# Differential attention stage: the second map is scaled on ScalarE, and its weights are split on ScalarE and VectorE instead of VectorE and GpSimd

## The chip, the core and the metric

The kernel runs on one core of one Trainium2 chip. The metric is device time in microseconds of one execution; the kernel before takes 766.11 us (median of 3 runs, 764.81 to 767.35). In the profile's names PE is TensorE's matmul stream and PEld its weight loads, DVE is VectorE, ACT is ScalarE, POOL is GpSimd and SP is the engine that issues the DMAs.

## The reference

One decoder layer on a sequence of 512 tokens, width 1024, in float32. The input is RMS-normalised and projected; two attention branches follow, latent attention with 8 heads ("MLA") and differential attention with 4 heads ("diff"). Each branch is projected to 1024 channels and multiplied by a sigmoid gate. The sum goes through an output projection and a residual; a SwiGLU feed-forward block with its own residual and a final norm end the layer. The part that the change touches is this one:

```python
o1 = causal_attention(dq[..., 0, :], dk[..., 0, :], dv)
o2 = causal_attention(dq[..., 1, :], dk[..., 1, :], dv)
lam = exp(sum(lambda_q1 * lambda_k1)) - exp(sum(lambda_q2 * lambda_k2)) + lambda_init
o_diff = rmsnorm(o1 - lam * o2, diff_subln_g) * (1.0 - lambda_init)
gates = sigmoid(gate_pre + b_gate)
merged = g_mla * (o_mla @ w_branch_mla) + g_diff * (o_diff @ w_branch_diff)
```

## The kernel before

**Numbers in two parts.** TensorE multiplies in the type float32r, which holds fewer bits than float32. Each operand is therefore kept as a rounded high part and a low part (the rest), and `mm3` (lines 298 to 302) issues three matmuls for one product: high by high (L300), high by low (L301), low by high (L302).

**Weights.** `weights` (from L270) loads a block of up to 128 x 1024 numbers by DMA into a `raw` tile (four buffers), and makes a `w` tile (three buffers) from it: `round_hi` (L261) writes the high part, `round_lo` (L267) subtracts it from the raw numbers to get the low part. A list of two names, `w_eng`, says which engine does which. In the first part of the program it is `['act', 'pool']`. From the MLA heads on it is `['dve', 'pool']`: the high part is a cast on VectorE at L265, the low part a subtraction on GpSimd at L268. In the feed-forward block it is `['act', 'dve']`: ScalarE at L263 and VectorE at L268. A block feeds 24 matmuls of 512 columns, and its buffer can be written again when the last of them is through.

**The differential heads.** `diff_head` goes over four blocks of 128 query rows; block i has (i+1) x 128 key columns. `scores` (from L623) makes both maps of a block on TensorE (L632) into two PSUM buffers (`ps_sc`, just two). VectorE adds the mask and takes the row maximum (L636), which writes the map to a `P` tile in SBUF and frees the PSUM buffer; ScalarE takes the exponential and its row sum (L155); VectorE takes the reciprocal of the sum (L639). Then the second map is multiplied by its reciprocal and by minus lambda (L684, VectorE), and the first map, multiplied by its own reciprocal, is added to it (L685, VectorE). TensorE transposes the result (L658), and the values are multiplied in `values` (L669). `diff_norm` (from L699) normalises a head; its sums over partitions run on TensorE (L703).

**What else runs there.** While the heads run, `fill` puts projections between their matmuls: those of the later diff heads (`diff_qk`, whose rotary part uses L563 and L564 on VectorE and L565 and L566 on GpSimd) and of the gates (`gate`, emptied from PSUM at L487). When all heads are through, `sigmoids` runs 16 sigmoids on ScalarE (L494), with a load of the function table ahead of them and one behind. Then come the branch projections: `branch(0, m)` and `branch(1, m)` for m = 0, 2, 4, 6, each from one block of weights; L797 multiplies a result with its gate.

**What sets the order.** Each engine works through its own list in order. The lists are written by a scheduler ahead of the run, by its own estimates of the durations and with priorities (`urgent` puts a head's work first); waits between the engines are semaphores. So another duration or another engine for one instruction can change the lists of all engines.

Of the kernel before, what the change touches and what calls it, by code (L numbers as in the profile page):

```python
# [16 lines left out]
AF = mybir.ActivationFunctionType  # L17
ALU = mybir.AluOpType
# [28 lines left out]
P_POOL = (0, 1)  # L47
W_ENG0 = ['act', 'pool']
W_ENG = ['dve', 'pool']
FILL = [[("gate", 0, 0)], [], [("pe", 0), ("mr", 0), ("gate", 0, 1), ("mv", 0)]]  # L50
FILL_MLA = [[("mqk", 1), ("mr", 1), ("v", 0), ("pe", 1)],
            [("mqk", 2), ("mr", 2), ("v", 1), ("mv", 1)],
# [40 lines left out]
def build(ctx, nc, tc, a, out):  # L93
# [9 lines left out]
    def T(tag, shape, dtype):  # L103
        return sb.tile(shape, dtype, name=nm(tag), tag=tag, bufs=BUFS[tag])
# [4 lines left out]
    def L_():  # L109
        return T("L", [P, 2, S], F32R)  # L110
# [4 lines left out]
    def tmp():  # L115
        return T("t", [P, S], F32)
# [4 lines left out]
    def r32(ap):  # L121
        return ap.bitcast(F32)
# [136 lines left out]
    w_eng = list(W_ENG0)  # L259
# [130 lines left out]
    neg_lam = sb.tile([P, 1], F32, name="neg_lam")  # L390
# [32 lines left out]
    for src in (turn_c, turn):  # L423
        tg = tmp()
        nc.gpsimd.memset(tg, 0.0)
        for q in range(4):
            with tc.issue_after(last_sin.ins):
                last_sin = nc.scalar.activation(out=tg[32 * q:32 * q + 32, q * P:(q + 1) * P],
                                                in_=src[32 * q:32 * q + 32, :], func=AF.Sin, scale=TWO_PI)
# [22 lines left out]
    def latent_norm(b):  # L452
        c0, ncol = ((0, QR), (QR, KVR))[b]
        nc.vector.tensor_mul(out=lat_ss[b], in0=lat_ss[b], in1=x_ms)
        rs = rsqrt(lat_ss[b], ncol, NB)
        nc.vector.tensor_mul(out=rs, in0=rs, in1=x_rs)
        for t in range(NB):
            l = latn[t][:, c0:c0 + ncol]
            nc.vector.tensor_scalar(out=l, in0=l, scalar1=rs[:, t:t + 1], scalar2=None, op0=ALU.mult)
            if b == 1:  # L460
                l = latn[t][:, c0 + ncol:c0 + ncol + RD]
                nc.vector.tensor_scalar(out=l, in0=l, scalar1=x_rs[:, t:t + 1], scalar2=None, op0=ALU.mult)
# [4 lines left out]
    def latents(n):  # L467
        for b in range(len(lat), n):
            pt = PS("tr")
            for t in range(NB):  # L470
                nc.tensor.transpose(out=pt[:, t * P:(t + 1) * P], in_=latn[t][:, b * P:(b + 1) * P], identity=ident)
            l = L_()
            split(pt, l[:, 0, :], l[:, 1, :], col(R_QG + b))
            lat.append(l)
# [25 lines left out]
    def fill(work):  # L500
        for kind, *args in work:
            if kind == "gate":
                gate(*args)
            elif kind == "v":
                diff_v(*args)
            elif kind == "qk":
                qk[args[0]] = diff_qk(*args)
            elif kind == "pe":
                pe[args[0]] = mla_pe(*args)
            elif kind == "mv":  # L510
                mv[args[0]] = mla_v(*args)
            elif kind == "mqk":
                mqk[args[0]] = mla_qk(*args)
            elif kind == "mr":
                mla_rope(args[0], mqk[args[0]], pe[args[0] // 2])
# [36 lines left out]
    latent_norm(1)  # L552
    fill(FILL[0])

    latents(5)
    fill(FILL[1])

# [56 lines left out]
    def rope_key():  # L614
        pt = PS("tr")
        for t in range(NB):
            nc.tensor.transpose(out=pt[0:RD, t * P:(t + 1) * P], in_=latn[t][:, 640:672], identity=ident)
        kpe = L_()[0:RD]
        rope(pt[0:RD, :], kpe[:, 0, :], kpe[:, 1, :], cos_m, sin_m, shuf_m, 1.0, RD)
        return kpe  # L620


    def scores(maps, i):  # L623


        n = (i + 1) * P
        pss = [PS("sc") for _ in maps]
        last = len(maps[0][0]) - 1
        for j in range(last + 1):
            for ps, (products, _) in zip(pss, maps):  # L630
                q, k = products[j]
                nc.tensor.matmul(out=ps[:, :n], lhsT=q[:, i * P:n], rhs=k[:, 0:n], start=j == 0, stop=j == last)  # L632
        rs = []
        for ps, (_, m) in zip(pss, maps):
            neg_max, s, r = sm(), sm(), sm()
            nc.vector.tensor_tensor_reduce(out=m, in0=ps[:, :n], in1=mask[:, S - n:], scale=-1.0, scalar=3.4e38,  # L636
                                           op0=ALU.add, op1=ALU.min, accum_out=neg_max)
            last_exp[0] = log_exp(out=m, in_=m, func=AF.Exp, bias=neg_max, scale=-1.0, accum_out=s)
            nc.vector.reciprocal(out=r, in_=s)  # L639
            rs.append(r)  # L640
        return rs

    def prob_tiles():
        c = T("P", [P, S], F32)
        yield c[:, 0:P]
        yield c[:, P:3 * P]
        for i in (2, 3):
            yield T("P", [P, S], F32)[:, :(i + 1) * P]

    def transposed(blocks):  # L650

        pt = T("PT", [P, 2, 1280], F32R)
        for js in ((0,), (1,), (2, 3)):
            ps = PS("tr")
            c = 0
            for j in js:
                for i in range(j, NB):
                    nc.tensor.transpose(out=ps[:, c:c + P], in_=blocks[i][:, j * P:(j + 1) * P], identity=ident)  # L658
                    c += P
            o0 = OFF[js[0]]  # L660
            split(ps[:, :c], pt[:, 0, o0:o0 + c], pt[:, 1, o0:o0 + c])
        return pt

    def values(pt, v):

        ps = PS("pv")
        for n_, (vs, s) in enumerate(((0, 0), (0, 1), (1, 0))):
            for j in range(NB):
                nc.tensor.matmul(out=ps[:, j * P:S], lhsT=v(j, vs), rhs=pt[:, s, OFF[j]:OFF[j] + S - j * P],  # L669
                                 start=n_ == 0 and j == 0, stop=n_ == 2 and j == NB - 1)  # L670
        return ps
# [7 lines left out]
    def diff_head(h, products):  # L679
        blocks = []  # L680
        for i, p1 in enumerate(prob_tiles()):
            p2 = T("P", [P, S], F32)[:, :(i + 1) * P]
            r1, r2 = scores(list(zip(products, (p1, p2))), i)
            nc.vector.tensor_scalar(out=p2, in0=p2, scalar1=r2, scalar2=neg_lam, op0=ALU.mult, op1=ALU.mult)  # L684
            nc.vector.scalar_tensor_tensor(out=p1, in0=p1, scalar=r1, in1=p2, op0=ALU.mult, op1=ALU.add)  # L685
            blocks.append(p1)
        pt = transposed(blocks)
        ps = values(pt, lambda j, s: dv[(h // 2) * 2 + j // 2][:, s, (j % 2) * 256 + (h % 2) * P:
                                                              (j % 2) * 256 + (h % 2) * P + P])
        o32, sq = tmp(), tmp()  # L690
        nc.scalar.activation(out=o32, in_=ps, func=AF.Copy)
        nc.scalar.activation(out=sq, in_=ps, func=AF.Square)
        sqs = L_()
        sqs = [sqs[:, 0, :], sqs[:, 1, :]]
        nc.vector.tensor_copy(out=sqs[0], in_=sq)
        nc.gpsimd.tensor_sub(out=sqs[1], in0=sq, in1=r32(sqs[0]))
        return o32, sqs

    def diff_norm(o32, sqs):  # L699

        ps = PS("tr")
        for s in range(2):
            nc.tensor.matmul(out=ps, lhsT=ones_r, rhs=sqs[s], start=s == 0, stop=s == 1)  # L703
        y, u = tmp(), tmp()
        log_exp(out=y, in_=ps, func=AF.Ln, scale=1.0 / P, bias=eps)
        last_exp[0] = log_exp(out=y, in_=y, func=AF.Exp, scale=-0.5)
        nc.vector.scalar_tensor_tensor(out=u, in0=ps, scalar=P * EPS, in1=y, op0=ALU.add, op1=ALU.mult)
        nc.vector.scalar_tensor_tensor(out=u, in0=u, scalar=-0.5 / P, in1=y, op0=ALU.mult, op1=ALU.mult)
        nc.gpsimd.tensor_mul(out=o32, in0=o32, in1=y)
        nc.vector.scalar_tensor_tensor(out=u, in0=u, scalar=1.5, in1=o32, op0=ALU.add, op1=ALU.mult)  # L710
        o = L_()
        split(u, o[:, 0, :], o[:, 1, :], col(R_SG))
        return o
# [88 lines left out]
    kpe = rope_key()  # L802
    fill(FILL[2])
    o_mla = []
    for p in range(4):
        o = L_()
        o_mla.append(o)
        w_eng[:] = W_ENG
        fill(FILL_MLA[p])
# [3 lines left out]


    o_diff, parts = [], []
    for h in range(4):
        fill(FILL_DIFF[h])
        with urgent():
            if h > 0:
                o_diff.append(diff_norm(*parts[h - 1]))  # L820
            parts.append(diff_head(h, qk[h]))
# [176 lines left out]
```

## Time and profile before

| | us |
|---|---|
| median of 3 runs | 766.11 |
| the profiled execution's own time | 765.69 |
| its span, from the first to the last instruction | 763.9 |
| PE busy | 738.9 (97%) |
| DVE busy | 430.5 (56%) |
| ACT busy | 293.4 (38%) |
| POOL busy | 166.9 (22%) |

The 1.8 us between the execution's time and its span lie outside the instructions. A share over the whole span hides the stages: from about 420 us on, the feed-forward block keeps TensorE busy and the others half idle, while in the stretch from 150 to 290 us, where the last MLA heads and the four diff heads run, VectorE is nearly always busy. A matmul's record is longer than the distance to the next one, so that a short wait of TensorE does not show as idle time. Where a row names a releaser behind an arrow, it is the instruction that ended the wait.

### The profile page before, as it was taken

The page shows a single profiled execution, that of the slowest core. Times are in us where ns is not written, and L with a number is a line of the kernel's source. Part 1 is how long each engine was busy: PE and PEld are TensorE (multiplying, and loading weights), DVE is VectorE, ACT ScalarE, POOL GpSimd, SP SyncE. Part 2 cuts the span into 40 slices and gives each one's busy share as a digit, 9 for nine tenths or more (in the row PEclk, how much of TensorE's full clock was granted, in tenths as well). Part 3 has the DMA queues.
Part 4 walks back from the last instruction along what each step waited for, and adds up shares of the span by engine and source line. Part 5 has one row for each costly group of instructions (what it writes and reads, how often), then busy time and mean ns, then how long its engine had stood idle before and what let it go on. Part 6 is the DMA issues. An engine that isn't in the chain of part 4 may idle for free.

```text
span 763.9 us, 9613 instructions
## 1 busy us (share of the span) xinstructions
PE 738.9 (97%) x3639; PEld 620.5 (81%) x3639; DVE 430.5 (56%) x800; ACT 293.4 (38%) x567; POOL 166.9 (22%) x120
## 2 busy tenths in 40 slices
PE   7999999999898999999999999999999999999996
PEld 5888889887686788888889888888888888888885
DVE  6968698898999983578363333233323332213424
ACT  7464658554333421724243323222222223122314
POOL 3404343564664454430000000000000000000302
PEclk9999999999999999999999999999999999999999
DMA  9405343632422322327422332323232323232302
GB/s 305 113 1 133 88 122 88 151 85 58 108 70 69 84 83 82 111 87 254 102 83 73 94 110 83 110 83 111 83 110 83 111 83 110 85 108 84 111 0 110
DMA packets 99819, 76.72 MB, mean 100 GB/s; under 512 B 6303, under 2 KB 86973, under 8 KB 99773
## 3 DMA queue, kind: packets, MB, share of 16 engines
q1 hardware_dynamic: 99773, 76.12, 34.0%
q8 instruction: 28, 0.46, 0.2%
q14 instruction: 18, 0.15, 0.1%
HBM read 69.81 MB, written 2.10 MB: 94 GB/s over the span
## 4 chain that ended last, share of the span: by engine, by line
PE 80%; DVE 13%; issue 2%; ACT 1%; POOL 1%; DMA 1%; SPq 0%; DVEq 0%; POOLq 0%; ACTq 0%
PE ps_mm L301 22%; PE ps_mm L302 22%; PE ps_mm L300 22%; PE ps_sc L632 2%; DVE L L256 2%; PE ps_sc L300 1%; PE ps_sc L301 1%; PE ps_tr L301 1%; PE ps_tr L300 1%; PE ps_tr L302 1%; PE ps_sc L302 1%; DVE L L254 1%; PE ps_tr L658 1%; DVE w L265 1%; DVE P L684 1%
## 5 line engine op out<-in xcount | busy, mean ns | idle before, releaser
L302 PE MATMUL ps_mm<-X,w 128*128 128x512 f32 (+1 forms) x568 | 217.6, 383 | 0.0
L300 PE MATMUL ps_mm<-X,w 128*128 128x512 f32 (+1 forms) x568 | 217.3, 383 | 0.2 <-DVE t L564 0.2
L301 PE MATMUL ps_mm<-X,w 128*128 128x512 f32 (+1 forms) x568 | 217.3, 383 | 0.0
L268 DVE TENSOR_TENSOR w<-raw,w 128x1024 fp32r<-128x1024 f32 x66 | 82.3, 1248 | 161.1 <-ACT w L263 161.0
L263 ACT ACTIVATE w<-raw 128x1024 fp32r<-128x1024 f32 (+1 forms) x72 | 74.0, 1029 | 160.1 <-issue 78.9
L268 POOL TENSOR_TENSOR w<-raw,w 128x1024 fp32r<-128x1024 f32 (+3 forms) x48 | 102.5, 2139 | 118.3 <-DVE w L265 36.3
L300 PEld LDWEIGHTS ps_mm<-X,w 128*128 128x128 f32 x568 | 107.1, 189 | 20.3 <-DVE t L564 0.4
L301 PEld LDWEIGHTS ps_mm<-X,w 128*128 128x128 f32 x568 | 107.2, 189 | 19.9 <-DVE X L254 0.2
L302 PEld LDWEIGHTS ps_mm<-X,w 128*128 128x128 f32 x568 | 107.1, 189 | 20.0 <-POOL w L268 0.3
L933 POOL TENSOR_TENSOR L<-L,P 128x512 f32<-128x512 f32 (+1 forms) x9 | 11.5, 1297 | 410.2 <-ACT t L932 410.1
L155 ACT ACTIVATE P<-P,sm 128x128 f32<-128x128 f32 (+3 forms) x64 | 35.9, 561 | 60.1 <-DVE sm L636 59.9
L907 DVE TENSOR_TENSOR t<-t,ps_mm 128x512 f32<-128x512 f32 x22 | 15.1, 688 | 59.7 <-PE ps_mm L302 59.7
L632 PE MATMUL ps_sc<-L,L 96*128 96x128 f32 (+7 forms) x160 | 38.0, 334 | 8.7 <-DVE sm L636 8.6
L906 ACT ACTIVATE t<-ps_mm 128x512 f32<-128x512 f32 x22 | 13.2, 598 | 80.8 <-PE ps_mm L302 80.8
L632 PEld LDWEIGHTS ps_sc<-L,L 96*128 96x128 f32 (+1 forms) x160 | 26.1, 191 | 14.6 <-DVE sm L636 12.3
L301 PE MATMUL ps_mm<-w,L 128*128 128x512 f32 (+1 forms) x100 | 37.2, 372 | 0.0
L300 PE MATMUL ps_mm<-w,L 128*128 128x512 f32 (+1 forms) x100 | 37.2, 374 | 0.0
L302 PE MATMUL ps_mm<-w,L 128*128 128x512 f32 (+1 forms) x100 | 37.1, 373 | 0.0
L265 DVE CAST w<-raw 128x1024 fp32r<-128x1024 f32 (+3 forms) x42 | 35.9, 855 | 1.6 <-PE ps_mm L302 1.1
L250 ACT ACTIVATE L<-t 64x512 fp32r<-64x512 f32 (+2 forms) x47 | 29.1, 624 | 17.0 <-POOL t L566 7.4
L301 PE MATMUL ps_mm<-L,w 128*128 128x512 f32 x90 | 35.5, 394 | 0.0
L254 DVE TENSOR_TENSOR L<-t,L 128x512 fp32r<-128x512 f32 (+2 forms) x37 | 33.1, 896 | 4.0 <-ACT L L250 3.7
(264 smaller groups left out, 1269.0 us busy)
## 6 DMA issues: line engine op xcount, KB each, us to landing
raw<-w_in SPq DMA_DIRECT2D x28, 512.0 KB, 4.0
raw<-w_ffn_gate SPq DMA_DIRECT2D x22, 512.0 KB, 3.9
raw<-w_ffn_up SPq DMA_DIRECT2D x22, 512.0 KB, 3.9
raw<-w_ffn_down SPq DMA_DIRECT2D x22, 512.0 KB, 3.6
L<-L SPq DMA_DIRECT2D x32, 128.0 KB, 2.3
raw<-w_out SPq DMA_DIRECT2D x8, 512.0 KB, 3.6
L<-x SPq DMA_DIRECT2D x8, 256.0 KB, 5.1
raw<-w_branch_mla SPq DMA_DIRECT2D x4, 512.0 KB, 3.4
```

Of the source, the lines that this page charges most:

```text
L155: return nc.scalar.activation(**kw)
L250: nc.scalar.activation(out=hi, in_=src, func=AF.Copy, scale=scale)
L254: nc.vector.tensor_sub(out=lo, in0=src, in1=r32(hi))
L256: nc.vector.scalar_tensor_tensor(out=lo, in0=src, scalar=scale, in1=r32(hi), op0=ALU.mult, op1=ALU.subtract)
L263: nc.scalar.activation(out=o, in_=i, func=AF.Copy)
L265: nc.vector.tensor_copy(out=o, in_=i)
L268: (nc.vector if w_eng[1] == 'dve' else nc.gpsimd).tensor_sub(out=o, in0=i, in1=r32(hi))
L300: nc.tensor.matmul(out=o, lhsT=lh, rhs=rh, start=start, stop=False)
L301: nc.tensor.matmul(out=o, lhsT=lh, rhs=rl, start=False, stop=False)
L302: return nc.tensor.matmul(out=o, lhsT=ll, rhs=rh, start=False, stop=stop)
L632: nc.tensor.matmul(out=ps[:, :n], lhsT=q[:, i * P:n], rhs=k[:, 0:n], start=j == 0, stop=j == last)
L907: nc.vector.tensor_mul(out=g, in0=g, in1=ps)
```

## The change

The second map is scaled in two steps. VectorE multiplies the 128 reciprocals by minus lambda (one column), and ScalarE multiplies the map by that column. From the program's first diff head on, `w_eng` is `['act', 'dve']`: 26 blocks of weights (18 of the projections between the heads, 8 of the branches) get their high part on ScalarE and their low part on VectorE.

```diff
@@ -47,6 +47,7 @@
 P_POOL = (0, 1)
 W_ENG0 = ['act', 'pool']
 W_ENG = ['dve', 'pool']
+W_ENG_DIFF = ['act', 'dve']
@@ -681,7 +682,8 @@
         for i, p1 in enumerate(prob_tiles()):
             p2 = T("P", [P, S], F32)[:, :(i + 1) * P]
             r1, r2 = scores(list(zip(products, (p1, p2))), i)
-            nc.vector.tensor_scalar(out=p2, in0=p2, scalar1=r2, scalar2=neg_lam, op0=ALU.mult, op1=ALU.mult)
+            nc.vector.tensor_mul(out=r2, in0=r2, in1=neg_lam)
+            nc.scalar.activation(out=p2, in_=p2, func=AF.Copy, scale=r2)
             nc.vector.scalar_tensor_tensor(out=p1, in0=p1, scalar=r1, in1=p2, op0=ALU.mult, op1=ALU.add)
             blocks.append(p1)
@@ -813,6 +815,7 @@
     o_diff, parts = [], []
+    w_eng[:] = W_ENG_DIFF
     for h in range(4):
```

The inserted lines shift the numbers: what is L268 before is L269 after, L636 is L637, and so on. Two places show how the lists move.

The first place is VectorE in the first diff head, at the block of 384 columns. Before (`P_2282` and `P_2283` are the two maps, `w_2415` is a block of weights, `ISA` is the masked maximum of L636):

```order
L636 ISA P_2282,sm_2290<-ps_sc_2284,mask 128x384
L636 ISA sm_2290 128x1
L254 TENSOR_TENSOR PT_2086<-ps_tr_2100,PT_2086 128x384
L265 CAST w_2415<-raw_2413 128x1024
L639 RECIPROCAL sm_2292<-sm_2291 128x1
L636 ISA P_2283,sm_2296<-ps_sc_2285,mask 128x384
L636 ISA sm_2296 128x1
L639 RECIPROCAL sm_2298<-sm_2297 128x1
L684 TENSOR_SCALAR P_2283<-P_2283,sm_2298,neg_lam 128x384
L685 SCALAR_TENSOR_TENSOR P_2282<-P_2282,sm_2292,P_2283 128x384
```

In the changed kernel (the same maps are `P_2284` and `P_2285`, and `w_2419` the same block of weights):

```order
L640 RECIPROCAL sm_2294<-sm_2293 128x1
L637 ISA P_2285,sm_2298<-ps_sc_2287,mask 128x384
L637 ISA sm_2298 128x1
L687 SCALAR_TENSOR_TENSOR P_2239<-P_2239,sm_2271,P_2262 128x256
L640 RECIPROCAL sm_2300<-sm_2299 128x1
L685 TENSOR_TENSOR sm_2300<-sm_2300,neg_lam 128x1
L255 TENSOR_TENSOR PT_2086<-ps_tr_2100,PT_2086 128x384
L687 SCALAR_TENSOR_TENSOR P_2284<-P_2284,sm_2294,P_2285 128x384
L637 ISA P_2307,sm_2315<-ps_sc_2309,mask 128x512
L637 ISA sm_2315 128x1
L269 TENSOR_TENSOR w_2419<-raw_2417,w_2419 128x1024
```

The map's scaling is gone from the list and a multiplication of one column stands in its place; the combination (L687) stands further from its reciprocal, since ScalarE works in between; the cast has become a subtraction. On ScalarE the same place now reads:

```order
L156 ACTIVATE P_2285,sm_2299<-P_2285,sm_2298 128x384
L251 ACTIVATE PT_2086<-ps_tr_2100 128x384
L686 ACTIVATE P_2285<-P_2285,sm_2300 128x384
L264 ACTIVATE w_2419<-raw_2417 128x1024
L156 ACTIVATE P_2307,sm_2316<-P_2307,sm_2315 128x512
L156 ACTIVATE P_2308,sm_2322<-P_2308,sm_2321 128x512
```

The scaling (L686) and a block's high part (L264) stand between the exponentials (L156).

The second place is ScalarE around the sigmoids. Before, the end of the sigmoids is followed by the last head's split (L252) and by splits of merged results (L250):

```order
L494 ACTIVATE L_3048<-L_3048,cols 128x512 x2
L494 ACTIVATE L_3111<-L_3111,cols 128x512 x2
L151 ACT_TABLE_LOAD
L252 ACTIVATE L_3296<-t_3289,cols 128x512
L250 ACTIVATE L_3482<-L_693 128x512
```

In the changed kernel, first what stands ahead of the sigmoids (`w_3334`, `w_3367` and `w_3400` are the blocks of `branch(0, 0)`, `branch(0, 2)` and `branch(0, 4)`), then what stands behind them (`w_3433` is that of `branch(0, 6)`, `w_3466` and the next those of `branch(1, ...)`):

```order
L264 ACTIVATE w_3334<-raw_3332 128x1024
L264 ACTIVATE w_3367<-raw_3365 128x1024
L253 ACTIVATE L_3167<-t_3160,cols 128x512
L264 ACTIVATE w_3400<-raw_3398 128x1024
L156 ACTIVATE t_3304<-ps_tr_3301,eps 128x512
L156 ACTIVATE t_3304<-t_3304 128x512
L495 ACT_TABLE_LOAD
```

```order
L495 ACTIVATE L_3123<-L_3123,cols 128x512 x2
L152 ACT_TABLE_LOAD
L253 ACTIVATE L_3312<-t_3305,cols 128x512
L264 ACTIVATE w_3433<-raw_3431 128x1024
L264 ACTIVATE w_3466<-raw_3464 128x1024
L264 ACTIVATE w_3507<-raw_3505 128x1024
```

Three of the four blocks of the first branch get their high part ahead of the sigmoids, the fourth behind the second table load. TensorE's list now begins that block with the four matmuls that need its high part alone:

```order
L303 MATMUL ps_mm_3417<-L_1870,w_3400 128x512
L301 MATMUL ps_mm_3436<-L_866,w_3433 128x512
L302 MATMUL ps_mm_3436<-L_866,w_3433 128x512
L301 MATMUL ps_mm_3450<-L_866,w_3433 128x512
L302 MATMUL ps_mm_3450<-L_866,w_3433 128x512
L303 MATMUL ps_mm_3436<-L_866,w_3433 128x512
```

Before, the low part was asked for by the block's third matmul:

```order
L302 MATMUL ps_mm_3401<-L_1870,w_3384 128x512
L300 MATMUL ps_mm_3420<-L_866,w_3417 128x512
L301 MATMUL ps_mm_3420<-L_866,w_3417 128x512
L302 MATMUL ps_mm_3420<-L_866,w_3417 128x512
L300 MATMUL ps_mm_3420<-L_1216,w_3417 128x512
```

On GpSimd the 26 subtractions of L268 are gone; the rotary steps, L696 and L709 stay. No DMA is added or removed.

## The prediction

> **What bounds the kernel now.** I read the busy times by stretch first, since a share over the whole span says nothing of one stage. The columns are the stretch, its length, then busy time (and instructions) of PE, PEld, DVE, ACT and POOL, granted clock, DMA share and GB/s.
>
> ```profile
> 80.00:150.00 70.00, 69.71 (x466) 64.23 (x466) 56.45 (x145) 46.24 (x110) 28.31 (x27) 1.00 0.39 104
> 150.00:290.00 140.00, 130.46 (x624) 105.97 (x623) 127.02 (x250) 57.18 (x135) 73.73 (x40) 0.99 0.33 84
> 290.00:345.00 55.00, 55.00 (x248) 45.67 (x247) 29.05 (x43) 21.53 (x34) 23.82 (x11) 1.00 0.30 95
> ```
>
> In the stretch of the last MLA heads and the diff heads TensorE is idle for 9.54 us of 140, and VectorE is busy for 127 of them. Before it (80 to 150) VectorE is busy for 81% and TensorE idle for 0.29 us; behind it TensorE has no gap. TensorE's waits in that stretch name the engine:
>
> ```profile
> PE ps_sc L632 <- DVE sm L636: 7.1, 6, 1.5
> PE ps_tr L658 <- DVE P L685: 2.0, 1, 2.0
> ```
>
> It waits for VectorE to empty a score buffer, or to combine two maps. The chain of waits agrees; VectorE has 13% of the span on it, 99 us:
>
> ```profile
> PE 80%; DVE 13%; issue 2%; ACT 1%; POOL 1%; DMA 1%; SPq 0%; DVEq 0%; POOLq 0%; ACTq 0%
> ```
>
> Why VectorE is late shows in the timelines (start, duration, engine, line), laid beside each other for two of these gaps, with an undisturbed row of the same form as the last:
>
> ```profile
> 180.12 2.38 POOL L268 TENSOR_TENSOR w<-raw,w 128x1024 fp32r<-128x1024 f32 x1 [4.44 <-DVE w L265]
> 180.43 2.61 DVE L254 TENSOR_TENSOR L<-t,L 64x512 fp32r<-64x512 f32 x1
> 183.50 0.62 PE L632 MATMUL ps_sc<-L,L 128*128 128x384 f32 x2 [1.48 <-DVE sm L636]
> 204.44 2.36 POOL L268 TENSOR_TENSOR w<-raw,w 128x1024 fp32r<-128x1024 f32 x1 [4.36 <-DVE sm L639]
> 204.55 2.80 DVE L685 SCALAR_TENSOR_TENSOR P<-P,sm,P 128x512 f32<-128x512 f32 x1
> 207.41 0.44 PE L658 MATMUL ps_tr<-ident,P 128*128 128x128 f32 x2 [1.99 <-DVE P L685]
> 255.18 0.73 DVE L685 SCALAR_TENSOR_TENSOR P<-P,sm,P 128x512 f32<-128x512 f32 x1
> ```
>
> A VectorE operation that starts behind a GpSimd subtraction ends when that is over: 2.80 us where the same form takes 0.73. It holds what stands behind it in VectorE's list, and TensorE stops.
>
> The lost time is more than the idle 9.54 us. Matmuls start 0.227 us apart but are recorded at 0.39, which hides 0.16 us of each gap: with nine gaps about 1.4 us. After the longest gap some eight matmuls start 0.42 us apart, which costs 8 x 0.19 = 1.5 us (the clock of 0.99 over the stretch).
>
> ```profile
> 299.83 0.39 PE L302 MATMUL ps_mm<-X,w 128*128 128x512 f32 x1
> 300.06 0.39 PE L300 MATMUL ps_mm<-X,w 128*128 128x512 f32 x1
> 208.96 0.63 PE L300 MATMUL ps_mm<-X,w 128*128 128x512 f32 x1
> 209.38 0.63 PE L301 MATMUL ps_mm<-X,w 128*128 128x512 f32 x1
> ```
>
> So 9.5 + 1.4 + 1.5 = 12.4 us are lost there, and TensorE's own work is 140 - 12.4 = 127.6 us, the same as VectorE's 127.0. This stage is bound by VectorE; 12.4 us is all there is to win.
>
> A page of the Trainium skill, "TensorE: Matmul & The Clock Gate" (HAM oscillation), puts the slow clock down to gaps over some 3.4 us. No gap here is longer than about 2.4 us, and the spacing doubled all the same. By that rule the 1.5 us would not come back, and the sum below would give 1.5 us less.
>
> **The change part by part.** The prices, from the groups of 150 to 345 us for the new forms from the feed-forward block (L268 and L263) and the MLA heads (L772 and L155), where they run already, and as the last the casts of 290 to 345 us alone:
>
> ```profile
> L265 DVE CAST w<-raw 128x1024 fp32r<-128x1024 f32 x26 | 21.4, 823 | 0.1
> L684 DVE TENSOR_SCALAR P<-P,sm,neg_lam 128x128 f32<-128x128 f32 x4 | 3.3, 816 | 0.1
> L684 DVE TENSOR_SCALAR P<-P,sm,neg_lam 128x256 f32<-128x256 f32 x4 | 2.3, 580 | 0.1
> L684 DVE TENSOR_SCALAR P<-P,sm,neg_lam 128x384 f32<-128x384 f32 x4 | 8.1, 2023 | 0.1
> L684 DVE TENSOR_SCALAR P<-P,sm,neg_lam 128x512 f32<-128x512 f32 x4 | 2.9, 734 | 0.0
> L639 DVE RECIPROCAL sm<-sm 128x1 f32<-128x1 f32 x38 | 6.0, 157 | 6.2 <-ACT P L155 6.1
> L268 DVE TENSOR_TENSOR w<-raw,w 128x1024 fp32r<-128x1024 f32 x52 | 63.7, 1226 | 138.4 <-ACT w L263 138.4
> L263 ACT ACTIVATE w<-raw 128x1024 fp32r<-128x1024 f32 x52 | 55.0, 1059 | 129.9 <-issue 74.9 <-PE ps_sc L302 38.3 <-PE ps_mm L302 12.4
> L772 ACT ACTIVATE P<-P,sm 128x512 f32<-128x512 f32 x6 | 4.3, 722 | 5.6 <-DVE sm L639 5.6
> L155 ACT ACTIVATE P<-P,sm 128x128 f32<-128x128 f32 x7 | 2.8, 397 | 4.6 <-DVE sm L636 4.6
> L268 POOL TENSOR_TENSOR w<-raw,w 128x1024 fp32r<-128x1024 f32 x26 | 65.2, 2509 | 60.8 <-DVE w L265 23.9 <-DVE sm L639 15.8 <-issue 10.2
> L566 POOL TENSOR_TENSOR t<-t,t 128x512 f32<-128x512 f32 x7 | 10.8, 1549 | 1.3 <-DVE t L564 1.2
> L265 DVE CAST w<-raw 128x1024 fp32r<-128x1024 f32 x8 | 5.5, 686 | 0.0
> ```
>
> *VectorE, scaling.* The 16 operations of L684 go: 3.3 + 2.3 + 8.1 + 2.9 = 16.6 us. Sixteen multiplications of one column come. None is in the trace; the reciprocal of one column is nearest, 16 x 0.157 = 2.5 us. Net -14.1.
>
> *VectorE, weights.* Of the 26 casts, the last eight lie behind 290 us and take 5.5 us, undisturbed; the 18 before take the other 15.9 of 21.4. They become subtractions, 18 x 1.226 = 22.1. Net +6.2.
>
> *VectorE, waiting behind GpSimd.* The other forms with 512 columns and two SBUF inputs carry the rest of the waits; undisturbed they take 0.68 us (the row at 201.45):
>
> ```profile
> 201.45 0.68 DVE L254 TENSOR_TENSOR L<-t,L 64x512 fp32r<-64x512 f32 x1
> L254 DVE TENSOR_TENSOR L<-t,L 64x512 fp32r<-64x512 f32 x12 | 12.8, 1065 | 0.6 <-ACT L L250 0.4
> L256 DVE SCALAR_TENSOR_TENSOR L<-t,L 64x512 fp32r<-64x512 f32 x7 | 10.9, 1564 | 0.3 <-ACT L L250 0.2
> L685 DVE SCALAR_TENSOR_TENSOR P<-P,sm,P 128x512 f32<-128x512 f32 x4 | 8.0, 1989 | 0.0
> L708 DVE SCALAR_TENSOR_TENSOR t<-t,t 128x512 f32<-128x512 f32 x4 | 5.5, 1381 | 0.0
> ```
>
> 12 x 0.38 + 7 x 0.88 + 4 x 1.31 + 4 x 0.70 = 18.8 us. GpSimd is busy for 97.5 us from 150 to 345, and 65.2 of that go; of the waits I take the same two thirds, 12.6 us. What stays on GpSimd (32 us in 195) can still hold up the new subtractions: at most one in six, for about a microsecond, some 3 us.
>
> Sum for VectorE from 150 to 290: -14.1 + 6.2 - 12.6 + 3 = -17.5, that is 109.5 us of work beside TensorE's 127.6, or 86%, between the 81% of the stretch where TensorE lost 0.3 us in 70 and the 91% recorded now.
>
> *ScalarE* takes 18 x 1.06 = 19.1 us and the scaled maps, four each of about 0.40, 0.5, 0.6 and 0.72 us (the rows of 128 and 512 columns, the two between by interpolation), 8.9 us. Its 57.2 us become 85 of some 130, 65%; from 80 to 150 it had 46.2 of 70, 66%, and TensorE did not wait. The work is hidden there, but two things stand in line: an exponential behind a 1.06 us conversion, and VectorE's subtraction and combination behind ScalarE's results. What they cost TensorE no row shows. Bounds: the 0.6 us that the rate of the stretch from 80 to 150 gives over 140, and the whole 28 us of ScalarE's added work laid on the path. I take 3 us, near the lower end, because that stretch mixed the same engines at the same loads.
>
> *The sigmoids.* Here the change takes cover away. A cast on VectorE did not care that ScalarE is shut for 14 us; now the fourth block of the first branch does.
>
> ```profile
> 308.68 1.28 ACT L494 ACT_TABLE_LOAD   x1
> 309.98 9.93 ACT L494 ACTIVATE L<-L,cols 128x512 f32<-128x512 f32 x16
> 319.92 1.28 ACT L151 ACT_TABLE_LOAD   x1
> 321.22 0.72 ACT L252 ACTIVATE L<-t,cols 128x512 fp32r<-128x512 f32 x1
> 305.73 0.39 PE L300 MATMUL ps_mm<-L,w 128*128 128x512 f32 x1
> ```
>
> In this profile's times: the branch begins at 305.7, and three converted blocks last 72 x 0.227 + 0.23 (one L703 in between) = 16.6 us, to 322.3. ScalarE is free at 321.9 and has the fourth high part at 323.0: 0.7 us of wait. Four matmuls need only that and last 0.9 us, to 323.9; the low part is there at 323.0 + 1.23 = 324.2, another 0.3. That makes 1.0 us, at best 0, and 2.5 if the order ahead of it slips by one more conversion and its subtraction. The blocks behind it come 1.06 us apart for 5.4 us of matmuls each, and are hidden.
>
> *DMAs* keep their number; a `raw` buffer is freed by VectorE where GpSimd freed it, and SP's list has only neighbours swapped. Hidden by the blocks loaded ahead: nothing.
>
> **Sum.** -12.4 + 3 + 1.0 = -8.4 us, on the profiled execution's 765.69 (span 763.9, the 1.8 us around it unchanged): 757.3. The median of the runs is 0.4 above that execution, so 757.7.
>
> **Rivals.**
>
> (a) *VectorE stays the bound.* The waits go with the number of GpSimd instructions, not their time, and the new subtractions are themselves operations with two SBUF inputs, nearly twice as long as the casts. Then half of the 12.4 us stays, as part of which the 3 us above count, and the sigmoids take their 1.0: -6.2 + 1.0 = -5.2, 760.9 us; with the half clock staying too (1.5), 762.4. Against it: the longest of them that stay (L566) take 1.55 us, not 2.5.
>
> (b) *The gain is given back.* The handovers cost what the waits cost, some 10 us instead of 3, and with the sigmoids nothing remains: 766 us. For it: the scheduler wrote all lists anew by estimates of its own, and those put TensorE into these waits before.
>
> (c) *Slower, by ScalarE's queue.* In each block of rows the exponentials stand behind conversions, and the scaling is one more trip to ScalarE before the transposes. All 28 us exposed, less 12.4, is +15.6; it turns to a loss when over 11.4 us of the 28 (41%) lie on the path beside the 1 us of the sigmoids. At half, +14 + 1 - 12.4 = +2.6, 768.7 us. Against it: ScalarE waited for others for most of this stretch, and TensorE has projections to do between scores.
>
> The Trainium skill's "ScalarE: Activation LUTs" (Rules for kernel authors) speaks for (c): multiplies and adds belong on VectorE, which is faster per element. The rows agree on the price alone (a high part takes 1.06 us on ScalarE, 0.68 undisturbed on VectorE); by that rule 26 x 0.38 = 10 us more would be spent, if the path went through ScalarE.
>
> **How the numbers follow.** Forecast 0.60 (753 to 760 us), (a) 0.16 (760 to 763.8), (b) 0.13, (c) 0.11. A change of 0.3%, 2.3 us, is about what a measurement can tell from none: below 763.8 faster, 0.60 + 0.16 = 0.76; (b) same, 0.13; (c) slower, 0.11. The range begins at all 12.4 us won and nothing lost, 753.5, rounded to 753, and ends at 765.5, with all of (a) and a little of (b) in it.
>
> **What would show it.** Right: no GpSimd row of 2.4 us in the stage; L687 at 512 columns near 0.73 us; TensorE's idle time from 150 to 290 down from 9.5 to 2 or 3 us, with no stretch at half clock; a gap of about 1 us behind the second table load, released by ScalarE's or VectorE's conversion. Wrong: waits of TensorE for L637 or L687 of the old total, VectorE's idle time released by ScalarE (L264 or L686), or a gap of several microseconds at the sigmoids.

## The result, and the profile after

The changed kernel takes 751.86 us (median of 6 runs, 751.41 to 753.9) against 765.16 us of the kernel before in 6 runs (764.81 to 767.35): 0.9825 of its time, with an interval of 0.9809 to 0.984, or 13.3 us less. A second set on another occasion gave 752.24 against 765.48 us, 0.9823 [0.9802, 0.9844]. What was said ahead of that one:

> The changed kernel once more, on the chip of the next three, so that a difference of one microsecond can be read. Every theory expects 751.9 us, within 751.4 to 752.5. Its first profile had two stretches at a lower granted clock (0.83 and 0.85) in code that the change does not touch; without them the span should be about 750 instead of 752.1 us.

The time came out so, with a span of 750.9. The forecast was 757.7 us with a range of 753 to 765.5: faster, as said, but by more than the range allowed.

The rows here are from the profiled execution of that second set (752.71 us, span 750.9); the first one has two stretches at a lower granted clock in code that the change does not touch; the last section comes back to one of them. First the busy times by stretch, with the columns of the prediction's table:

```profile
80.00:150.00 70.00, 69.72 (x466) 64.22 (x466) 56.43 (x144) 46.24 (x110) 28.33 (x27) 1.00 0.40 105
150.00:290.00 140.00, 139.90 (x689) 117.38 (x688) 113.30 (x256) 86.73 (x174) 33.67 (x23) 1.00 0.34 92
290.00:345.00 55.00, 54.44 (x239) 44.39 (x238) 40.18 (x60) 34.02 (x51) 1.29 (x1) 1.00 0.37 122
```

From 150 to 290 us TensorE is idle for 0.10 us, where it was 9.54; GpSimd's busy time has fallen from 73.73 to 33.67, ScalarE's risen from 57.18 to 86.73, VectorE's fallen from 127.02 to 113.30. The chain of waits has lost 5 points of VectorE and gained 2 of ScalarE:

```profile
PE 86%; DVE 8%; ACT 3%; issue 1%; DMA 1%; POOL 1%; SPq 0%; DVEq 0%; ACTq 0%
```

Who waits for whom has turned round. The groups of VectorE and ScalarE in that stretch (busy us, mean ns of one, idle time ahead and its releaser):

```profile
L269 DVE TENSOR_TENSOR w<-raw,w 128x1024 fp32r<-128x1024 f32 x20 | 26.8, 1340 | 3.2 <-ACT w L264 3.2
L488 DVE TENSOR_TENSOR L<-ps_mm,x_rms 128x512 f32<-128x512 f32 x13 | 8.8, 686 | 10.6 <-PE ps_mm L303 10.6
L685 DVE TENSOR_TENSOR sm<-sm,neg_lam 128x1 f32<-128x1 f32 x16 | 3.2, 198 | 0.3
L687 DVE SCALAR_TENSOR_TENSOR P<-P,sm,P 128x512 f32<-128x512 f32 x4 | 3.0, 743 | 1.5 <-ACT P L686 1.5
L264 ACT ACTIVATE w<-raw 128x1024 fp32r<-128x1024 f32 x20 | 21.1, 1055 | 13.6 <-PE ps_mm L303 13.6
```

VectorE now waits 10.6 us for TensorE ahead of L488, ScalarE 13.6 us ahead of its conversions: both run ahead of TensorE. Behind ScalarE VectorE does wait, 3.2 us for high parts and 1.5 us for the scaled maps of 512 columns, but in time that it has to spare. The combination of 512 columns takes 0.743 us, where it took 1.989.

To place the gain I take three instructions that both programs have: the first score matmuls of an MLA head near 75 us, the first branch matmul, and the first matmul of the output projection. Before:

```profile
75.04 0.85 PE L632 MATMUL ps_sc<-L,L 96*128 96x128 f32 x6
305.73 0.39 PE L300 MATMUL ps_mm<-L,w 128*128 128x512 f32 x1
349.51 0.39 PE L300 MATMUL ps_mm<-w,L 128*128 128x512 f32 x1
```

After:

```profile
75.13 0.85 PE L633 MATMUL ps_sc<-L,L 96*128 96x128 f32 x6
291.62 0.39 PE L301 MATMUL ps_mm<-L,w 128*128 128x512 f32 x1
336.55 0.39 PE L301 MATMUL ps_mm<-w,L 128*128 128x512 f32 x1
```

The heads last 230.69 us before and 216.49 after, 14.20 less; the branches 43.78 and 44.93, 1.15 more. Together 13.05, of 13.0 between the two spans (763.9 and 750.9): nothing else moved.

### The profile page after: what moved, and what is told of

Same layout as the page of the kernel before. It is cut to its first block, busy times and chain, and to the rows that moved or that the text cites. A ratio compares the mean times of both kernels' runs of the same rounds, so it can differ in the third digit from the quotient of the medians.

```text
span 752.1 us, 9652 instructions
## 1 busy us (share of the span) xinstructions
PE 737.0 (98%) x3639; PEld 623.0 (83%) x3639; DVE 414.7 (55%) x800; ACT 326.8 (43%) x609; POOL 104.3 (14%) x94
## 4 chain that ended last, share of the span: by engine, by line
PE 81%; DVE 9%; ACT 5%; POOL 2%; issue 2%; DMA 1%; SPq 0%; DVEq 0%; ACTq 0%
PE ps_mm L301 22%; PE ps_mm L303 22%; PE ps_mm L302 22%; PE ps_sc L633 2%; PE ps_sc L301 1%; PE ps_sc L302 1%; PE ps_tr L301 1%; PE ps_tr L302 1%; PE ps_tr L303 1%; PE ps_sc L303 1%; POOL t L567 1%; PE ps_tr L659 1%; ACT L L495 1%; DVE w L269 1%; DVE X L355 1%
## 5 line engine op out<-in xcount | busy, mean ns | idle before, releaser
L269 DVE TENSOR_TENSOR w<-raw,w 128x1024 fp32r<-128x1024 f32 x92 | 116.3, 1266 | 165.4 <-ACT w L264 165.2
L264 ACT ACTIVATE w<-raw 128x1024 fp32r<-128x1024 f32 (+1 forms) x98 | 101.1, 1036 | 181.2 <-issue 78.9
L909 ACT ACTIVATE t<-ps_mm 128x512 f32<-128x512 f32 x22 | 13.2, 598 | 80.9 <-PE ps_mm L303 80.9
L156 ACT ACTIVATE P<-P,sm 128x128 f32<-128x128 f32 (+3 forms) x64 | 35.8, 560 | 27.4 <-DVE sm L637 27.0
L269 POOL TENSOR_TENSOR w<-raw,w 128x1024 fp32r<-128x1024 f32 (+3 forms) x22 | 37.3, 1701 | 57.5 <-PE ps_tr L472 25.8
L301 PE MATMUL ps_mm<-L,w 128*128 128x512 f32 x90 | 35.2, 393 | 0.5 <-ACT w L264 0.5
L302 PE MATMUL ps_mm<-L,w 128*128 128x512 f32 x90 | 35.5, 394 | 0.0
L303 PE MATMUL ps_mm<-L,w 128*128 128x512 f32 x90 | 35.2, 393 | 0.0
L251 ACT ACTIVATE L<-t 64x512 fp32r<-64x512 f32 (+2 forms) x47 | 29.1, 623 | 13.6 <-POOL t L567 6.2
L255 DVE TENSOR_TENSOR L<-t,L 128x512 fp32r<-128x512 f32 (+2 forms) x37 | 29.6, 801 | 4.8 <-ACT L L251 4.5
```

Source lines behind the costliest of these rows:

```text
L156: return nc.scalar.activation(**kw)
L251: nc.scalar.activation(out=hi, in_=src, func=AF.Copy, scale=scale)
L255: nc.vector.tensor_sub(out=lo, in0=src, in1=r32(hi))
L264: nc.scalar.activation(out=o, in_=i, func=AF.Copy)
L269: (nc.vector if w_eng[1] == 'dve' else nc.gpsimd).tensor_sub(out=o, in0=i, in1=r32(hi))
L301: nc.tensor.matmul(out=o, lhsT=lh, rhs=rh, start=start, stop=False)
```

## The experiments

The theory is that GpSimd's subtractions held up VectorE's operations (the "hold"); its main rival is that VectorE simply had too much to do (the "load"). The table has the median, the ratio to the kernel before on the same chip, and the two distances between the landmarks above. The edits below are shown against the changed kernel, the last but one against the scaling alone, and shortened to the lines that matter.

| kernel | us | ratio [95%] | heads | branches |
|---|---|---|---|---|
| before | 765.15, 765.48 | | 230.69 | 43.78 |
| the change | 752.24 | 0.9823 [0.9802, 0.9844] | 216.49 | 44.93 |
| weights alone | 753.79 | 0.9842 [0.9818, 0.9865] | 217.76 | 44.91 |
| scaling alone | 769.04 | 1.0042 [1.0028, 1.0056] | 233.91 | 43.78 |
| high parts alone on ScalarE | 764.73 | 0.9988 [0.9976, 1.0] | 227.42 | 45.69 |
| GpSimd repeats the subtractions | 770.59 | 1.0062 [1.004, 1.0085] | 233.22 | 46.93 |
| branch high parts on VectorE | 751.26 | 0.981 [0.9788, 0.9832] | 216.48 | 43.78 |
| scaling alone, scalar operand | 767.39 | 1.0029 [1.0016, 1.0042] | 232.79 | 43.78 |
| both parts on VectorE | 755.89 | 0.987 [0.9848, 0.9891] | 222.33 | 43.77 |

The distances come from one profiled execution each (for the change, that of the second set), and in some a stretch at half clock lies within the heads (two in "scaling alone, scalar operand", one in before and in three others); so small differences are read from the medians.

**One half of the change at a time.** First the weights alone:

```diff
-            nc.vector.tensor_mul(out=r2, in0=r2, in1=neg_lam)
-            nc.scalar.activation(out=p2, in_=p2, func=AF.Copy, scale=r2)
+            nc.vector.tensor_scalar(out=p2, in0=p2, scalar1=r2, scalar2=neg_lam, op0=ALU.mult, op1=ALU.mult)
```

> The weights' split moved as in the change, the second map scaled on VectorE as before. Theory (the hold): VectorE loses its time behind GpSimd's 2.4 us subtractions, and those are gone here, so most of the gain comes: 752 to 757 us, TensorE idle under 3 us of the stage. Rival (the load): VectorE's plain work decides; the subtractions add 6.2 us to it (18 x 1.226 - 15.9) and nothing of its own is taken away, so no gain or a loss: 763 to 771 us.

Then the scaling alone, with the weights as before:

```diff
-    w_eng[:] = W_ENG_DIFF
```

> The second map scaled on ScalarE as in the change, the weights split on VectorE and GpSimd as before. The hold: all 26 GpSimd subtractions stay, what stands behind them on VectorE is held as before, so less than half of the gain: 759 to 764 us, with VectorE rows of 2 us and more left. The load: VectorE gives up 14.1 us of 127, more than the 12.4 us that TensorE lost by the prediction's count, so nearly all of the gain: 752 to 755 us.

The weights alone take 753.79 us: 11.4 of the 13.3 us. The scaling alone makes the kernel slower by 3.9 us, which neither theory expected, although VectorE is busy for 9.5 us less from 150 to 290 us. Stretches of the two, weights first:

```profile
150.00:290.00 140.00, 139.30 (x683) 115.93 (x682) 115.34 (x255) 77.97 (x156) 33.73 (x23) 1.00 0.34 90
```

```profile
150.00:290.00 140.00, 128.13 (x608) 101.39 (x607) 117.54 (x246) 64.58 (x149) 71.78 (x39) 1.00 0.31 80
L684 DVE TENSOR_TENSOR sm<-sm,neg_lam 128x1 f32<-128x1 f32 x16 | 9.4, 585 | 0.4
```

VectorE has nearly the same load in both, 115 and 118 us; TensorE is idle for 0.7 us in the one and 11.9 in the other. The load does not decide. The second row shows what is new: a multiplication of 128 numbers takes 585 ns on average beside GpSimd's subtractions, 198 ns without them. The average mixes two kinds: ten of the 16 take 0.15 to 0.16 us; the other six, each begun while a GpSimd operation ran, take 0.67 to 2.24 us and end within 0.03 us of that operation's end.

**High parts alone on ScalarE, low parts still on GpSimd.** This takes the casts off VectorE and leaves GpSimd's work; the scaling is as before.

```diff
-W_ENG_DIFF = ['act', 'dve']
+W_ENG_DIFF = ['act', 'pool']
```

> High parts on ScalarE, low parts still on GpSimd, the second map scaled on VectorE as before. VectorE gives up 18 casts (15.9 us) in the stage and gets nothing for them, while every GpSimd subtraction stays. The hold: a gain of at most a third, 760 to 765 us. The load: VectorE falls to 111 us beside TensorE's 127.6, so most of the gain, 752 to 756 us.

```profile
150.00:290.00 140.00, 133.24 (x641) 108.81 (x640) 109.07 (x233) 74.97 (x156) 73.28 (x40) 0.99 0.32 85
PE ps_sc L633 <- DVE sm L637: 5.4, 5, 2.5
```

VectorE's load is the lowest of all kernels here, 109.07 us, and TensorE still stops for 6.76 us, mostly where VectorE should empty a score buffer; the time is 764.73 us, as the hold theory had it (760 to 765) and not the load theory (752 to 756). Between the landmarks (a half clock lies in both profiles) it wins 3.3 us in the heads and gives 1.9 back in the branches, where the block behind the sigmoids waits for a high part from ScalarE (0.5 us) and a low part from GpSimd (0.8 us). Even without these 1.9 us it would lie at 762.8, far from 752 to 756: the load theory falls with this run.

**GpSimd made busy again.** The changed kernel, in which GpSimd repeats each of the 26 subtractions into a tile that nothing reads.

```diff
+        if again[0]:
+            nc.gpsimd.tensor_sub(out=spare, in0=i, in1=r32(hi))
```

> The changed kernel, and GpSimd makes each of the 26 subtractions once more into a tile that nothing reads (the results are left out of the computation), so that only its 2.4 us instructions come back. The hold: much of the loss returns, 757 to 765 us, with VectorE operations of two SBUF inputs at 2 us and more. The load: VectorE's own work is that of the changed kernel, 751 to 753 us.

```profile
150.00:290.00 140.00, 128.52 (x612) 103.37 (x611) 126.95 (x247) 80.43 (x168) 79.60 (x39) 0.99 0.31 80
L274 DVE TENSOR_TENSOR w<-raw,w 128x1024 fp32r<-128x1024 f32 x17 | 31.0, 1826 | 1.5 <-ACT w L264 1.4
```

It takes 770.59 us, more than the kernel before. Nothing waits for these results, yet the gain is gone and more: VectorE's subtraction takes 1826 ns instead of 1340, and TensorE is idle for 11.5 us. I had said 757 to 765. The longer VectorE operations are seen directly; GpSimd's repeated subtraction takes 2.98 us on average, longer than the 2.51 us of the one before the change. How much of the overshoot comes from that, from the `raw` and `w` buffers, which here come free only behind GpSimd, and from the lists that the scheduler wrote anew, stays open.

**The sigmoids.** The changed kernel, with the branches' eight high parts as casts on VectorE.

```diff
+    w_eng[:] = ['dve', 'dve']
     sigmoids(last_exp[0], (0, 1))
```

> The changed kernel, but the eight blocks of the branch projections get their high part as a cast on VectorE, as before the change. Theory (the fourth block waits for ScalarE, which is shut for 14 us by the sigmoids and their two table loads): the 1.0 us comes back, no wait of TensorE for L264 or L269 near 310 us, and about 750.8 us. VectorE takes 8 x 0.69 = 5.5 us more between 290 and 345 us, where it has 15 us free. Rival (the lists after the heads are written anew, and the 1.1 us between branch start and output projection come from the order and not from the wait): 751.9 us or more.

In the changed kernel the place looks as foretold (start, duration, engine):

```profile
305.83 1.28 ACT L152 ACT_TABLE_LOAD   x1
307.76 2.94 ACT L264 ACTIVATE w<-raw 128x1024 fp32r<-128x1024 f32 x3
307.98 0.39 PE L303 MATMUL ps_mm<-L,w 128*128 128x512 f32 x1
308.86 0.50 PE L301 MATMUL ps_mm<-L,w 128*128 128x512 f32 x1 [0.49 <-ACT w L264]
309.66 0.40 PE L302 MATMUL ps_mm<-L,w 128*128 128x512 f32 x1
310.12 0.50 PE L303 MATMUL ps_mm<-L,w 128*128 128x512 f32 x1
```

The fourth block's first matmul starts 0.88 us behind the one ahead of it where 0.227 is the rule, a wait of 0.65; the first that needs the low part 0.46 behind, another 0.23. With the casts on VectorE this is gone: in the rows of 290 to 345 us TensorE is busy for 55.00 of 55, and the branches last 43.78 us again, to the hundredth what they lasted before the change.

```profile
290.00:345.00 55.00, 55.00 (x244) 45.53 (x243) 45.41 (x67) 28.05 (x45) 1.29 (x1) 1.00 0.38 126
```

The heads last 216.48 us, against 216.49. The median is 751.26 us against 752.24 of the change on the same chip: 1.0 less, the size of the 1.15 that the traces show, though the intervals of the two ratios overlap. It has the lowest median of all versions here.

**The one-column multiplication.** The scaling alone once more, with minus lambda as a scalar operand instead of a second input from SBUF.

```diff
-            nc.vector.tensor_mul(out=r2, in0=r2, in1=neg_lam)
+            nc.vector.tensor_scalar(out=r2, in0=r2, scalar1=neg_lam, scalar2=None, op0=ALU.mult)
```

> The scaling alone is moved to ScalarE, weights as before the change (that took 769.04 us), and the multiplication of the one column takes minus lambda as a scalar operand per partition instead of a second input of the same shape. Theory A (the column's multiplication has two SBUF inputs and is held by GpSimd's subtractions, 585 ns against 198 ns without them): L684 falls to 160 to 200 ns, and some of the 3.9 us lost comes back, 764 to 767.5 us. Theory B (the loss is the extra trip over ScalarE, and the holds of 16 such small operations cost nothing on the path): L684 may fall, but the time stays at 768.5 to 770 us.

```profile
L684 DVE TENSOR_SCALAR sm<-sm,neg_lam 128x1 f32<-128x1 f32 x16 | 3.4, 211 | 0.3
PE ps_sc L632 <- DVE sm L636: 5.2, 6, 1.5
PE ps_tr L704 <- DVE L L696: 3.0, 1, 3.0
```

The operation falls from 585 to 211 ns (first row; the others are TensorE's longest waits in the stage) beside the same GpSimd work, a little above the 160 to 200 of theory A. None of the 16 is held: they take 0.20 to 0.22 us, seven of them begun while a GpSimd operation ran. The loss falls from 3.9 to 1.9 us, at the edge of what A said; since the two intervals overlap, the size of this step is not settled. The other 1.9 us remain. That they are the extra trip over ScalarE is argued, not shown: the lists differ too. For the third head, TensorE's list has 11 matmuls between the values (L669) and the sum over partitions (L703) in the kernel before and none here, where the 3.0 us wait for L696 lies.

**Both parts on VectorE.** This separates "away from GpSimd" from "onto ScalarE".

```diff
-W_ENG_DIFF = ['act', 'dve']
+W_ENG_DIFF = ['dve', 'dve']
```

> The changed kernel, but with both parts of the 26 blocks on VectorE: the high part as a cast instead of on ScalarE. VectorE then has 18 x 0.82 = 15 us more work from 150 to 290 us than in the changed kernel, about 127 us, as much as before the change, and GpSimd has none of the subtractions. Theory hold (GpSimd's subtractions held up VectorE, and its load alone does not stop TensorE): 752 to 759 us, TensorE idle for at most 5 us of the 140. Rival load (VectorE was the bound by its busy time): 762 us or more, TensorE idle for 8 us or more.

755.89 us, as the hold theory said. VectorE's load came to 117.70 us and not to the expected 127. The casts took 14.5 us, about as expected, but the stretch holds fewer of the other operations than in the changed kernel, some of these are shorter, and records of operations in close succession overlap; so this run tests the load less sharply than meant. Beside the scaling alone it is sharp: the two kernels differ in the engine of the low parts only, VectorE has the same load in both (117.70 and 117.54 us), and the times are 755.89 and 769.04 us.

Against the change it loses 3.7 us. Here is the place where its heads lose most:

```profile
260.19 0.69 DVE L266 CAST w<-raw 128x1024 fp32r<-128x1024 f32 x1
260.41 0.99 PE L670 MATMUL ps_pv<-PT,L 128*128 128x256 f32 x6
260.79 0.61 DVE L687 SCALAR_TENSOR_TENSOR P<-P,sm,P 128x384 f32<-128x384 f32 x1
261.32 1.22 DVE L269 TENSOR_TENSOR w<-raw,w 128x1024 fp32r<-128x1024 f32 x1
261.93 0.59 ACT L694 ACTIVATE t<-ps_pv 128x512 f32<-128x512 f32 x1
262.45 0.69 DVE L637 CUSTOM_DVE_ANT_0 P<-ps_sc,mask 128x512 f32<-128x512 f32 x1
263.06 0.42 DVE L697 CAST L<-t 128x512 fp32r<-128x512 f32 x1
263.63 0.47 PE L705 MATMUL ps_tr<-L,ones_r 128*128 128x512 f32 x1 [2.24 <-DVE L L697]
```

No operation here is stretched. TensorE's list has nothing between the head's values (L670) and the sum over partitions (L705), where the changed kernel has 24 matmuls. So TensorE waits for the whole chain: ScalarE squares the values (L694, through at 262.52 us), VectorE rounds the squares (L697) behind one masked maximum (L637). The cast and the subtraction are through when the squares are there. The stop costs 2.35 us from start to start, and seven matmuls at half clock behind it about 1.4. Three shorter stops in the heads, 1.8 us together, wait for VectorE too. So the 3.7 us are what this version costs, but more through the order of TensorE's list than through plain load; how much of it ScalarE wins by shortening VectorE's queue is not shown.

**The runs in pairs.** Two pairs differ in the engine of the low parts alone: high parts alone against weights alone (764.73 and 753.79 us), and scaling alone against this run (769.04 and 755.89, from two sets of runs). Leaving GpSimd is worth 10.9 and 13.2 us in them, although VectorE gets the work. Moving the high parts to ScalarE is worth 0.4 us beside GpSimd's subtractions, hardly clear of nothing, and 3.7 without them. "Load" was wrong as the main cause.

## Why the prediction was right in kind and wrong in size

**The mechanism held.** VectorE's operations behind GpSimd's subtractions were the main loss: the four experiments in which GpSimd keeps, or gets back, a share of them as large as before lie between 764.7 and 770.6 us, the changed kernel and the three others without between 751.3 and 755.9.

**Step that failed: "I take 3 us" for the handovers between ScalarE and VectorE.** I chose it inside bounds of 0.6 and 28 us. The runs show none: TensorE is idle for 0.10 us in the stage, below even the lower bound (and from start to start a single stop of over 0.15 us is left, 0.26 us). The row that should have decided was the one that I cited, the stretch from 80 to 150 us with the same engines at the same loads and 0.29 us idle; I moved up from it for a risk that no row showed. That is 3.0 of the 5.8 us between 757.7 and 751.86.

**Second step: "12.4 us is all there is to win".** The heads became 14.2 us shorter. The step counted idle records, a hidden 0.16 us for each of them, and the half clock. It left out what hardly shows as idle. One such stop before the change:

```profile
235.49 0.39 PE L301 MATMUL ps_mm<-X,w 128*128 128x512 f32 x1
235.95 0.61 PE L632 MATMUL ps_sc<-L,L 128*128 128x384 f32 x2
```

The starts are 0.46 us apart where 0.227 is the rule: 0.23 us lost, 0.07 recorded as idle. I measured from start to start, from 150 us to the first branch matmul, against the median distance behind each form of matmul. The kernel before loses 15.9 us by that, the changed one 1.6: 14.2 less, as the landmarks say. Before, six stops of over half a microsecond make 9.8 us, the half clock 1.5, and four stops of 0.2 to 0.5 us 1.4, of which the changed kernel has one of 0.26 left. That is 12.4 us, about what the step had counted. The other 1.8 lie in distances that miss the median by less than 0.15 us each (a balance of 3.2 us before and 1.4 after); which of them are waits is not shown. As a bound it was the more serious fault: the lower end of the range, 753, was built on it, and the time fell 1.1 us below.

**Two slips in the sums.** With all 12.4 us won and nothing lost the forecast's sum gives 753.7 us, not 753.5. In rival (b), 10 us of handovers and 1.0 at the sigmoids leave 1.4 of the 12.4, so 764.7 us rather than 766. Neither changes the account.

**The base.** 766.11 was the median of three runs; with six it is 765.16, which makes up 0.95 us of the miss, within the spread of the runs.

**The sigmoids: right.** Predicted 1.0 us from 0.7 for the high part and 0.3 for the low; measured 0.65 and 0.23 in those two waits and 1.15 in all (two more distances there are 0.11 us too long), and taken away by the run that removes its cause.

**VectorE's sum.** 109.5 us predicted, 113.3 measured. The scaling's removal, the column multiplications (198 ns, taken as 157) and the combinations came as said; the stretch now takes in some 14 us more of the program, with 20 subtractions rather than 18, and the subtractions took 1340 ns, not 1226: four of the 20, each beside one of the operations that stayed on GpSimd, took 1.56 to 1.98 us, the others 1.22 to 1.24. So the 3 us allowed for this came out as 2.3. The share of VectorE did not matter, as TensorE waited for none of it. ScalarE's 85 us came out as 86.7, hidden.

**The rivals.** (a) failed: the waits went with GpSimd's long operations, and the subtractions on VectorE suffered little. (b) and (c) failed in the changed kernel. Where GpSimd keeps its work, the kernel with the scaling on ScalarE is slower, by 3.9 us in one form and 1.9 in the other, as (c) would have it; whether by the trip to ScalarE or by other lists is not shown. Without GpSimd's holds the same step seems to gain a little (753.79 to 752.24 or 751.86 us, with overlapping intervals; the heads are 1.27 us shorter). The Trainium skill, "ScalarE: Activation LUTs" (Rules for kernel authors), puts adds and multiplies on VectorE and gives its advantage per element for bf16. The scaling is such a multiply: the runs agree with the rule beside GpSimd's subtractions and show no loss without them. The high parts are conversions, which the rule does not name and to which the prediction stretched it; the version that keeps them on VectorE takes 3.7 us more.

## What to carry to other kernels

Where an operation's mean in one stage is two or three times its undisturbed row, look for the engine that it was held by before moving load about: taking 18 us off VectorE's busy time won 0.4 us here (3.3 in the heads, most of it lost again in the branches), taking GpSimd's subtractions away won 10.9 to 13.2. Count a bottleneck's lost time from start to start against the regular distance, not from its idle records, before calling it a bound. And where two engines of the same loads already run without a stop in a neighbouring stretch, take the price of the handover from that row first: here it was nearer than the guess. A run that moves one instruction also gets new lists; look at the place of the longest wait in both lists before giving the difference to the engine.

## What the hardware showed beyond that

**A small operation can be held as long as a large one.** The 128-number multiplication with two inputs from SBUF, behind a GpSimd subtraction (scaling alone):

```profile
210.26 2.40 POOL L268 TENSOR_TENSOR w<-raw,w 128x1024 fp32r<-128x1024 f32 x1 [3.89 <-DVE w L265]
210.44 2.24 DVE L684 TENSOR_TENSOR sm<-sm,neg_lam 128x1 f32<-128x1 f32 x1
```

With one input and a scalar operand, begun behind the same kind of subtraction, it is not held:

```profile
211.23 2.39 POOL L268 TENSOR_TENSOR w<-raw,w 128x1024 fp32r<-128x1024 f32 x1 [3.94 <-DVE w L265]
212.32 0.21 DVE L684 TENSOR_SCALAR sm<-sm,neg_lam 128x1 f32<-128x1 f32 x1
```

One input is no safeguard in general. The scaling of a whole map, in the kernel before, has one and two scalars; 0.54 us is its time for 512 columns undisturbed, and here it takes 2.58 for 384:

```profile
246.85 2.39 POOL L268 TENSOR_TENSOR w<-raw,w 128x1024 fp32r<-128x1024 f32 x1 [5.35 <-DVE sm L639]
246.88 2.58 DVE L684 TENSOR_SCALAR P<-P,sm,neg_lam 128x384 f32<-128x384 f32 x1
```

The Trainium skill, "SBUF — State Buffer" (Who interferes with whom), says that a VectorE instruction with two SBUF inputs contends with a GpSimd instruction that reads SBUF, that one with at most one SBUF input does not, outside VectorE's 2-port modes, and that casts and operations with scalars can enter these modes. The first two pairs of rows agree with the first two points; whether the map's scaling, held with one input, ran in a 2-port mode no run shows.

**Half clock comes with some executions of a gap and not with others.** Between 77.9 and 79.9 us every kernel here has a wait of about 1.5 us for the same row maximum. In the first profile of the changed kernel the matmuls behind it start 0.21 us apart for some 3 us:

```profile
78.80 0.79 PE L633 MATMUL ps_sc<-L,L 96*128 96x384 f32 x3 [1.47 <-DVE sm L637]
80.37 0.41 PE L301 MATMUL ps_mm<-w,X 128*128 128x256 f32 x1
80.58 0.41 PE L302 MATMUL ps_mm<-w,X 128*128 128x256 f32 x1
82.93 0.35 PE L301 MATMUL ps_mm<-w,X 128*128 128x256 f32 x1
```

In the second profile of the same program the wait is the same, and the matmuls start 0.12 us apart:

```profile
79.01 0.80 PE L633 MATMUL ps_sc<-L,L 96*128 96x384 f32 x3 [1.48 <-DVE sm L637]
80.01 0.28 PE L302 MATMUL ps_mm<-w,X 128*128 128x256 f32 x1
80.13 0.28 PE L303 MATMUL ps_mm<-w,X 128*128 128x256 f32 x1
```

In the run of the scaling with a scalar operand a wait of twice that length is followed by the regular 0.23 us:

```profile
275.83 0.48 PE L704 MATMUL ps_tr<-L,ones_r 128*128 128x512 f32 x1 [2.96 <-DVE L L696]
276.71 0.39 PE L301 MATMUL ps_mm<-X,w 128*128 128x512 f32 x1
276.93 0.39 PE L302 MATMUL ps_mm<-X,w 128*128 128x512 f32 x1
```

In the scaling alone, five waits of 1.3 to 2.1 us in the stage are followed by no half clock at all. So the 1.5 us at half clock that I put down to the longest gap is a draw of that execution as much as a property of the stage; in both profiles of the changed kernel the stage has none. The Trainium skill, "TensorE: Matmul & The Clock Gate" (HAM oscillation), asks for gaps of over some 3.4 us; here half clock followed waits of 1.5 to 2.5 us, and did not follow one of 3 us.
